# Moving an attention sub-norm's denominators, sums and power from VectorE to GpSimd, and leaving rows unscaled until one last multiply

## The chip, the core and the metric

The kernel runs on one core of a Trainium2 chip. The metric is the device time of one launch in microseconds (us), as the median of several runs. The engines are TensorE (PE in the profile; PEld its weight loads), VectorE (DVE), ScalarE (ACT), GpSimd (POOL), and SyncE (SP), which issues nearly all DMAs. Each engine works through its own list of instructions in order; semaphores tie the lists together.

## The reference, cut to what matters

A two-layer hybrid encoder over 1024 tokens and 16 meta tokens, model width 1024. In each layer half of the width goes through a Fourier mixer, the other half through four heads of differential attention; both are gated and projected back to the residual. What the change touches is the norm of each attention row `o` (128 wide), its gain and its gate:

```python
p = jax.nn.softmax(s, axis=-1)
a = p[:, :, 0] - lam_f * p[:, :, 1]
o = jnp.einsum('bhqk,bkhd->bqhd', a, vf)
...
o = rms_norm(o, subln_gain[li]) * (1.0 - lambda_init)   # o * rsqrt(mean(o*o) + 1e-6) * gain
a_out = o.reshape(b, l, V_WIDTH)
...
y = jnp.concatenate([f_out, a_out], axis=-1)
y = y * jax.nn.silu(gate)
```

## The kernel before

**Stages.** Each layer runs a Fourier stage (`fourier`), then per head a projection from the normed rows (`head_projection`, matmuls on line 545), then attention (`attention`), with other work put between the attention's steps by `fill`: the next head's projection, the projection back of the Fourier half (`out_fourier`) and, towards the end of a layer, that of the attention half (`phase_out`); the latter two share `out_tile` (matmuls L283, addition on DVE L290). Every fp32 operand is split into a high and a low part, and a product takes three matmuls.

**Attention.** A group is two query tiles of 128 rows (and, for the last group of a head in layer 0, the 16 meta rows) of one head; there are 16 groups in each layer. Per tile and for each of the two maps: six scores matmuls into a three-bank PSUM tile "S" (L633, L635); DVE evicts it with its running minimum (L640); ACT takes the exponential with the row's sum (L643). Then DVE takes a reciprocal of the second sum (L647), a factor (L649) and combines both maps into unscaled rows (L651). PE transposes these rows in eight steps and a remainder (L661, L669) into the "M" banks; ACT makes the high part (L666), DVE the low part (L667); the remainder goes through L672 and L673. After a group's last tile PE multiplies with the values (L681, L682) and ACT copies the result (`osb`, L684).

**Finish.** `finish` is called one group later, between later scores. It loads the stored gate (SP, `gt`, L692), transposes the group's output back to rows (PE L695, ACT L697), then works on a set: two tiles (32 sets), or the 16 meta rows alone (4 sets), 36 sets with 68 tile-rows in all. `ls` holds the row sums of the first map. On DVE r1 = 1/ls (L699); on ACT the sum of squares of the rows scaled by r1 (L703, one a tile); on DVE so/128 + eps (L705); on POOL the power of -0.5 (L707); on DVE times r1 (L708); on DVE, one a tile, gate times row times factor (L710); SP stores it (`yad`, L712). `phase_out` loads it back (`ya`, L780), PE transposes it into a "G" bank (L785), and ACT and DVE make high and low parts with the gain column `sgc` (`yh` L789, `yl` L790), which L283 multiplies with the last weights.

**Weights.** `Weights.split` (L172) turns fp32 weights into high (ACT, `wh`, L180) and low parts (DVE, `wl`, L181). They arrive through two staging buffers (`wst`, loads L165), so the third load of a set must wait for both halves of the first to be split.

**Order.** The instructions of each engine aren't in the order of the source. A scheduler with its own model of costs arranges them across all engines before the kernel is built, so an edit in one place can change the order everywhere behind it. PSUM gives three "M" banks, two "G" banks and one "S" tile.

Of the kernel before, what the change touches and what calls it, by code (L numbers as in the profile page):

```python
# [10 lines left out]
F32 = mybir.dt.float32  # L11
F32R = mybir.dt.float32r
AF = mybir.ActivationFunctionType
ALU = mybir.AluOpType
# [4 lines left out]
P = 128  # L19
# [11 lines left out]
EPS = 1e-6  # L31
# [17 lines left out]
def trunk(ctx: ExitStack, tc, x, meta, ngain, w_in, w_f, qg, kg, lq1, lk1, lq2, lk2, subg, w_out,  # L49
          ident_d, chan_d, rope_d, dft_d, dftt_d, out, dbg=None):  # L50
    nc = tc.nc
    pe, act, dve, pool, sp = nc.tensor, nc.scalar, nc.vector, nc.gpsimd, nc.sync
# [4 lines left out]
    sm = ctx.enter_context(tc.tile_pool(name="sm", bufs=3))  # L57
# [7 lines left out]
    def nm(s):  # L65
        uid[0] += 1
        return f"{s}_{uid[0]}"
# [4 lines left out]
    def bank():  # L72
        return psM.tile([P, 512], F32, tag="M", name=nm("M"))
# [22 lines left out]
    def tile_rows(t):  # L96
        return NMETA if t == NT else P
# [13 lines left out]
    sgc = cst.tile([P, DEPTH], F32, name="sgc")  # L111
# [3 lines left out]
    def lam_init(li):  # L115
        return 0.8 - 0.6 * math.exp(-0.3 * li)

    def small_constants(ini):
        W = DEPTH * HD
        lv = [ini.tile([P, 256], F32, tag="sq", name=nm("lv"), bufs=3) for _ in range(2)]  # L120
        for i, v in enumerate((lq1, lk1, lq2, lk2)):
            sp.dma_start(lv[i % 2][:, W * (i // 2):W * (i // 2) + W], v.rearrange("d h -> (d h)").partition_broadcast(P))
        pr = lv[0][:, 0:2 * W].rearrange("p (a c) -> p a c", a=2)
        dve.tensor_tensor(pr, pr, lv[1][:, 0:2 * W].rearrange("p (a c) -> p a c", a=2), op=ALU.mult)
        sums = sm.tile([P, 2 * DEPTH], F32, name="sums", bufs=1)
        dve.tensor_reduce(sums, pr.rearrange("p a (d h) -> p (a d) h", d=DEPTH), axis=AX.X, op=ALU.add)
        act.activation(sums, sums, AF.Exp)
        dve.tensor_tensor(lamb, sums[:, DEPTH:], sums[:, 0:DEPTH], op=ALU.subtract)
        for li in range(DEPTH):
            dve.tensor_scalar(lamb[:, li:li + 1], lamb[:, li:li + 1], lam_init(li), None, op0=ALU.subtract)  # L130
        for dst, g in ((kgc, kg), (qgc, qg)):
            pool.memset(dst, 1.0)
            for c in range(2):
                for li in range(DEPTH):
                    sp.dma_start(dst[HD * c + ROT:HD * c + HD, li:li + 1],
                                 g[li, ROT:HD].rearrange("(h o) -> h o", o=1))
        dve.tensor_scalar(qgc, qgc, HD ** -0.5, None, op0=ALU.mult)
        for li in range(DEPTH):
            sp.dma_start(sgc[:, li:li + 1], subg[li].rearrange("(h o) -> h o", o=1))
            dve.tensor_scalar(sgc[:, li:li + 1], sgc[:, li:li + 1], 1.0 - lam_init(li), 0.5,  # L140
                              op0=ALU.mult, op1=ALU.mult)

    def rope_tables(li, rp, rc):
# [156 lines left out]
    def fourier(li, hT, fo, ep, w, nxt):  # L300
# [116 lines left out]
        for gp in range(2):  # L417
# [20 lines left out]
            if gp == 0:  # L438
                channel_maps()
                with tc.issue_after(ins.ins):  # L440
                    rope_tables(li, ep, fo)
                    if li == 0:
                        small_constants(ep)
# [110 lines left out]
    def attention(li, wk, store, fill, marks, ready, progress):  # L554
# [13 lines left out]
        def group_tiles(gi):  # L568
            return [2 * gi, 2 * gi + 1] + ([NT] if gi == 3 and li < DEPTH - 1 else [])
# [117 lines left out]
        def finish(h, gi, osb, ls):  # L687
            sets = [(0, 2, P)] + ([(2, 1, NMETA)] if len(group_tiles(gi)) > 2 else [])
            for i0, n, R in sets:
                t0 = group_tiles(gi)[i0]  # L690
                gt = wk.tile([P, 2, P], F32, tag="gt", name=nm("gt"), bufs=1)
                sp.dma_start(gt[0:R, 0:n], gtd[li][h][t0:t0 + n, 0:R, :].rearrange("t p d -> p t d"))  # L692
                pb = bank()
                for i in range(n):
                    pe.transpose(pb[0:R, P * i:P * i + P], osb[:, P * (i0 + i):P * (i0 + i) + R], ident)  # L695
                ot = osb[:, 0:2 * P].rearrange("p (t d) -> p t d", t=2)
                act.copy(ot[0:R, 0:n], pb[0:R, 0:P * n].rearrange("p (t d) -> p t d", t=n))  # L697
                r1 = sm.tile([P, 2], F32, tag="r1", name=nm("r1"))
                dve.reciprocal(r1[0:R, 0:n], ls[0:R, i0:i0 + n])  # L699
                so = sm.tile([P, 2], F32, tag="so", name=nm("so"), bufs=2)  # L700
                sqo = wk.tile([P, P], F32, tag="sqo", name=nm("sqo"), bufs=1)
                for i in range(n):
                    act.activation(sqo[0:R], ot[0:R, i], AF.Square, scale=r1[0:R, i:i + 1],  # L703
                                   accum_out=so[0:R, i:i + 1])
                dve.tensor_scalar(so[0:R, 0:n], so[0:R, 0:n], 1.0 / P, EPS, op0=ALU.mult, op1=ALU.add)  # L705
                rs = sm.tile([P, 2], F32, tag="rso", name=nm("rso"), bufs=2)
                pool.tensor_tensor(rs[0:R, 0:n], so[0:R, 0:n], nhalf[0:R, 0:n], op=ALU.pow)  # L707
                dve.tensor_tensor(rs[0:R, 0:n], rs[0:R, 0:n], r1[0:R, 0:n], op=ALU.mult)  # L708
                for i in range(n):
                    dve.scalar_tensor_tensor(gt[0:R, i], ot[0:R, i], rs[0:R, i:i + 1], gt[0:R, i],  # L710
                                             op0=ALU.mult, op1=ALU.mult)
                    sp.dma_start(yad[li][t0 + i][0:R, P * h:P * h + P], gt[0:R, i])  # L712
                    if h == NH - 1:
                        ready.add(t0 + i)
# [6 lines left out]
        def flush_finish():  # L721
            if fin[0] is not None:
                finish(*fin[0])
                fin[0] = None
# [19 lines left out]
        for n, item in enumerate(items):  # L744
            h, gi, i, t = item
# [107 lines left out]
    with tc.tile_pool(name="in0", bufs=2, side="right", reuse_waits="tile") as wk:  # L853
        for t in list(range(MT)) + [NT] + list(range(MT, NT)):
            R = tile_rows(t)
# [145 lines left out]
```

## Time and profile before

| | us |
|---|---|
| median of 3 runs | 1213.92 |
| lowest and highest run | 1213.86, 1215.79 |
| the profiled execution, its own time | 1215.41 |
| its span (first to last instruction) | 1213.6 |
| granted PE clock, mean over the span | 0.994 of full speed |
| PE busy | 1163.2 |
| DVE busy | 833.5 |
| ACT busy | 675.9 |
| POOL busy | 148.5 |

The span is what the views below divide. 1.8 us of the profiled execution's time lie around its span. The table of busy times says which engine has the least room; the waits say whom that engine waited for; the timeline tells, at one place, which instruction stood in front of which.

### The profile page before, as it was taken

The numbers are of one execution on the slowest core, as the hardware profiler recorded it, in microseconds if no ns is written. First come the engines' busy times: TensorE is split into PE (matmuls) and PEld (weight loads), VectorE is DVE, ScalarE is ACT, GpSimd is POOL, SyncE is SP. The second block draws the span as 40 slices with busy tenths as digits, with TensorE's granted clock in tenths as the row PEclk, the third lists the DMA queues.
The fourth block names the chain that finished last, engine by engine and source line by source line (L and its number), as shares of the span: only waits on it lengthen the run. The fifth ranks groups of instructions, "written<-read, shape, count | busy, mean of one in ns | idle before, by whom it ended". The sixth has DMA issues, their size and how long they took to land.

```text
span 1213.6 us, 18701 instructions
## 1 busy us (share of the span) xinstructions
PE 1163.2 (96%) x6676; PEld 1001.6 (83%) x6676; DVE 833.5 (69%) x1803; ACT 675.9 (56%) x1644; POOL 148.5 (12%) x157
## 2 busy tenths in 40 slices
PE   6999999999999999999999999999999999999998
PEld 5999986877787787788879999877888888878786
DVE  6352546788788789888683525367787887987863
ACT  5332325677767667666453223356676776866740
POOL 1101023010211201100011000140111112101000
PEclk9999999999999998999999999999999999999899
DMA  7420303012012014744335202030120210473253
GB/s 236 134 70 18 91 28 101 7 31 77 14 47 61 14 32 148 221 150 131 134 127 167 70 19 90 29 100 8 43 58 23 57 49 20 143 220 128 101 159 117
DMA packets 103613, 105.46 MB, mean 87 GB/s; under 512 B 11233, under 2 KB 87585, under 8 KB 103265
## 3 DMA queue, kind: packets, MB, share of 16 engines
q1 hardware_dynamic: 103104, 99.59, 26.4%
q0 software_dynamic: 416, 4.70, 1.1%
q8 instruction: 52, 0.85, 0.3%
q14 instruction: 41, 0.33, 0.1%
HBM read 74.62 MB, written 29.62 MB: 86 GB/s over the span
## 4 chain that ended last, share of the span: by engine, by line
PE 80%; DVE 8%; ACT 6%; DMA 3%; issue 2%; POOL 1%; SPq 1%; ACTq 0%; DVEq 0%; POOLq 0%
PE G L545 23%; PE G L283 13%; PE G L349 8%; PE S L349 7%; PE M L681 7%; PE S L633 4%; PE S L635 4%; PE M L661 3%; PE S L545 3%; DVE p L640 2%; PE M L390 2%; ACT p L643 2%; DVE p L651 1%; DMA wst<-in_w_in_dram 1%; PE M L401 1%
## 5 line engine op out<-in xcount | busy, mean ns | idle before, releaser
L545 PE MATMUL G<-wh,hT 128*128 128x512 f32 x896 | 307.5, 400 | 2.8 <-ACT va L484 1.0
L545 PEld LDWEIGHTS G<-wh,hT 128*128 128x128 f32 x896 | 167.4, 188 | 42.9 <-ACT wh L180 1.9
L643 ACT ACTIVATE p<-p,mx 128x1040 f32<-128x1040 f32 x136 | 158.6, 1166 | 69.6 <-DVE p L640 68.4
L640 DVE TENSOR_SCALAR_CACHE_REDUCE p<-S 128x1040 f32<-128x1040 f32 x136 | 167.9, 1234 | 40.7 <-PE S L635 33.4
L545 PE MATMUL G<-wl,hT 128*128 128x512 f32 x448 | 176.4, 395 | 0.6 <-DVE wl L181 0.6
L283 PE MATMUL G<-wh,yh 128*128 128x512 f32 (+2 forms) x276 | 107.4, 402 | 6.5 <-ACT yh L789 4.0
L181 DVE TENSOR_TENSOR wl<-wst,wh 128x512 fp32r<-128x512 f32 x128 | 85.7, 701 | 29.5 <-ACT wh L180 29.2
L283 PE MATMUL G<-wl,yh 128*128 128x512 f32 (+2 forms) x276 | 105.8, 392 | 0.0
L180 ACT CAST wh<-wst 128x512 fp32r<-128x512 f32 x128 | 74.7, 620 | 52.5 <-DMA wst<-in_w_in_dram 23.5
L545 PEld LDWEIGHTS G<-wl,hT 128*128 128x128 f32 x448 | 84.3, 188 | 16.3 <-DVE wl L181 1.2
L349 PE MATMUL G<-hT,wh 128*128 128x384 f32 (+3 forms) x384 | 96.4, 331 | 0.0
L283 PE MATMUL G<-wh,yl 128*128 128x512 f32 (+1 forms) x260 | 93.0, 398 | 0.0
L499 POOL TENSOR_TENSOR rsq<-ss,nhalf 128x12 f32<-128x12 f32 x24 | 54.9, 2287 | 307.0 <-DVE ss L497 261.8
L349 PE MATMUL S<-hT,wh 128*128 128x256 f32 (+3 forms) x384 | 91.0, 321 | 1.4 <-DVE sg L437 1.3
L667 DVE TENSOR_TENSOR atl<-M,ath 128x512 fp32r<-128x512 f32 x136 | 86.2, 655 | 5.5 <-ACT ath L666 4.6
L651 DVE SCALAR_TENSOR_TENSOR p<-p,cc,p 128x1040 f32<-128x1040 f32 (+1 forms) x68 | 88.2, 1297 | 1.3
L635 PE MATMUL S<-k,ql 128*128 128x264 f32 (+3 forms) x408 | 88.1, 323 | 0.0
L666 ACT CAST ath<-M 128x512 fp32r<-128x512 f32 x136 | 72.7, 565 | 15.3 <-PE M L661 14.5
L661 PE MATMUL M<-ident,p 128*128 128x128 f32 x544 | 73.8, 271 | 0.1
L681 PE MATMUL M<-ath,vh 128*128 128x256 f32 (+1 forms) x256 | 73.4, 287 | 0.2 <-DVE atl L667 0.2
L681 PE MATMUL M<-ath,vl 128*128 128x256 f32 (+1 forms) x256 | 73.0, 285 | 0.0
L681 PE MATMUL M<-atl,vh 128*128 128x256 f32 (+1 forms) x256 | 72.8, 284 | 0.0
(193 smaller groups left out, 2408.1 us busy)
## 6 DMA issues: line engine op xcount, KB each, us to landing
wst<-in_w_in_dram SPq DMA_DIRECT2D x64, 192.0 KB, 2.8
xt<-in_x_dram SPq DMA_DIRECT2D x16, 512.0 KB, 3.9
wst<-in_w_in_dram SPq DMA_DIRECT2D x32, 256.0 KB, 4.5
wst<-in_w_out_dram SPq DMA_DIRECT2D x16, 512.0 KB, 4.3
xmid<-xt SPq DMA_DIRECT2D x16, 512.0 KB, 2.8
xt<-xmid SPq DMA_DIRECT2D x16, 512.0 KB, 4.6
tab<-in_dft_dram POOLq DMA_DIRECT2D x2, 2096.0 KB, 10.9
yfd<-sg SPq DMA_DIRECT2D x8, 520.0 KB, 2.7
```

What stands on the lines that cost most here:

```text
L180: act.copy(h, self.staged[q][:, j, :])
L181: dve.tensor_tensor(l, self.staged[q][:, j, :], f(h), op=ALU.subtract)
L283: pe.matmul(pb[0:m, 0:e - c], lhsT=a[:, k, 0:m], rhs=b[2 * k + n][:, c:e], start=k == 0 and i == 0, stop=k == 3 and i == n_pass - 1)
L349: pe.matmul(o, lhsT=w[k][:, c:c + P], rhs=hT[:, k, s, a:b], start=k == 0 and i == 0, stop=k == KT - 1 and i == 2)
L545: pe.matmul(pss[t][0:part.shape[-1], a:b], lhsT=part, rhs=w[k][:, a:b], start=k == 0 and i == 0, stop=k == KT - 1 and i == len(pairs) - 1)
L635: ins = pe.matmul(ps[0:R, C0 + a:C0 + b], lhsT=ql[:, qo:qo + R], rhs=kk[:, a:b], start=False, stop=True)
L640: dve.tensor_scalar(pc[0:R], ps[0:R, C0:C0 + L], -1.0, None, op0=ALU.mult, op1=ALU.min, accum_out=mx[0:R])
L643: act.activation(pc[0:R], pc[0:R], AF.Exp, bias=mx[0:R], scale=-1.0, accum_out=lc)
L651: dve.scalar_tensor_tensor(pp[0][0:R], pp[1][0:R], cc[0:R], pp[0][0:R], op0=ALU.mult, op1=ALU.add)
L661: pe.transpose(pb[:, R * j:R * j + R], pa[0:R, P * kt:P * kt + P], ident[0:R, 0:R])
L667: dve.tensor_tensor(atl[:, 4 * c:4 * c + 4, qo:qo + R], src, f(hi), op=ALU.subtract)
L681: pe.matmul(po[:, 0:w], lhsT=v[:, kt, :], rhs=a[:, kt, 0:w], start=kt == 0 and i == 0, stop=False)
```

## The change

Before, the rows were scaled by 1/ls for the sum of squares, and the factor of the norm was multiplied by 1/ls again. Now they stay unscaled: with q the sum of squares of the unscaled row, rsqrt(q/(128 ls²) + eps)/ls equals sqrt(128) · rsqrt(q + 128 · eps · ls²). POOL makes `el` = 128 · eps · ls² in two instructions (L700, L701), adds it to the sum of squares (L706) and raises it to -0.5 (L708); sqrt(128) goes into the constant `sgc` that L789 and L790 apply later. The Square on ACT (now L705) needs no scale. Three DVE instructions a set are gone (L699, L705, L708 of before), three POOL instructions a set are new: 108 of each. The DVE multiplication with the gate (L710) keeps its line.

```diff
-            dve.tensor_scalar(sgc[:, li:li + 1], sgc[:, li:li + 1], 1.0 - lam_init(li), 0.5,
+            dve.tensor_scalar(sgc[:, li:li + 1], sgc[:, li:li + 1], 1.0 - lam_init(li), 0.5 * math.sqrt(P),
...
-                r1 = sm.tile([P, 2], F32, tag="r1", name=nm("r1"))
-                dve.reciprocal(r1[0:R, 0:n], ls[0:R, i0:i0 + n])
+
+                el = sm.tile([P, 2], F32, tag="r1", name=nm("el"))[0:R, 0:n]
+                pool.tensor_tensor(el, ls[0:R, i0:i0 + n], ls[0:R, i0:i0 + n], op=ALU.mult)
+                pool.tensor_scalar(el, el, EPS * P, None, op0=ALU.mult)
                 so = sm.tile([P, 2], F32, tag="so", name=nm("so"), bufs=2)
                 sqo = wk.tile([P, P], F32, tag="sqo", name=nm("sqo"), bufs=1)
                 for i in range(n):
-                    act.activation(sqo[0:R], ot[0:R, i], AF.Square, scale=r1[0:R, i:i + 1],
-                                   accum_out=so[0:R, i:i + 1])
-                dve.tensor_scalar(so[0:R, 0:n], so[0:R, 0:n], 1.0 / P, EPS, op0=ALU.mult, op1=ALU.add)
+                    act.activation(sqo[0:R], ot[0:R, i], AF.Square, accum_out=so[0:R, i:i + 1])
+                pool.tensor_tensor(so[0:R, 0:n], so[0:R, 0:n], el, op=ALU.add)
                 rs = sm.tile([P, 2], F32, tag="rso", name=nm("rso"), bufs=2)
                 pool.tensor_tensor(rs[0:R, 0:n], so[0:R, 0:n], nhalf[0:R, 0:n], op=ALU.pow)
-                dve.tensor_tensor(rs[0:R, 0:n], rs[0:R, 0:n], r1[0:R, 0:n], op=ALU.mult)
```

The change also moves instructions that it doesn't touch, since the scheduler orders all of them anew. The engines' lists are the same up to layer 0's attention; PE keeps all of its instructions, in another order from there on. Three places follow.

On DVE, at the first finish of layer 0 (`att` and `gs` belong to the attention and to the next head's projection, `p_2511` is an eviction of scores):

```order
 L673 TENSOR_TENSOR att<-M_2448,att 16x128
-L705 TENSOR_SCALAR so_2400<-so_2400 128x2
 L480 SCALAR_TENSOR_TENSOR gs_2698<-gs_2698,G_2568 128x128
-L708 TENSOR_TENSOR rso_2405<-rso_2405,r_342_2398 128x2
+L710 SCALAR_TENSOR_TENSOR gt_2392<-osb_2369,rso_2406,gt_2392 128x128 x2
 L640 TENSOR_SCALAR p_2511,mx_2510<-S_2503 128x1040
-L710 SCALAR_TENSOR_TENSOR gt_2392<-osb_2369,rso_2405,gt_2392 128x128 x2
```

The multiplication with the gate moved ahead of the next eviction of scores.

On ACT, late in layer 1, where the last set of weights is split (`wst_12524` and `wst_12534` are the third and the fourth staging load of that set; `yh_12688` is the first tile of `phase_out`):

```order
 L180 CAST wh_12526<-wst_12524 128x512
 L180 CAST wh_12530<-wst_12524 128x512
+L789 ACTIVATE yh_12688<-G_12683,sgc 128x512
+L684 COPY osb_12364<-M_12338 128x256
 L180 CAST wh_12536<-wst_12534 128x512
 L180 CAST wh_12540<-wst_12534 128x512
-L789 ACTIVATE yh_12688<-G_12683,sgc 128x512
-L684 COPY osb_12364<-M_12338 128x256
+L697 COPY osb_12364<-M_12390 128x256
 L643 ACTIVATE p_12416,l_2289_12369<-p_12416,mx_12415 128x1040
-L697 COPY osb_12364<-M_12390 128x256
```

`yh_12688` and the copy of `osb` moved ahead of the two casts of the fourth load.

On DVE at the same place (`wl_12521` is the second half of the second load, whose buffer the fourth load needs):

```order
+L651 SCALAR_TENSOR_TENSOR p_12252<-p_12270,cc_12294,p_12252 128x1040
 L181 TENSOR_TENSOR wl_12521<-wst_11919,wh_12520 128x512
 L290 TENSOR_TENSOR xt_12544<-xt_12544,G_12555 128x512
 L673 TENSOR_TENSOR att<-M_12322,att 16x128
 L290 TENSOR_TENSOR xt_12544<-xt_12544,G_12556 128x512
-L651 SCALAR_TENSOR_TENSOR p_12252<-p_12270,cc_12294,p_12252 128x1040
-L699 RECIPROCAL r_2358_12652<-ls_12242 128x2
 L181 TENSOR_TENSOR wl_12527<-wst_12524,wh_12526 128x512
```

The combination of two maps moved ahead of `wl_12521`, and so ahead of what frees the fourth load's buffer.

## Rows read from the trace of the kernel before

**Rows 1.** The page, busy time, share of the span, instructions of each engine.

```profile
PE 1163.2 (96%) x6676; PEld 1001.6 (83%) x6676; DVE 833.5 (69%) x1803; ACT 675.9 (56%) x1644; POOL 148.5 (12%) x157
```

**Rows 2.** The page, the chain that ended last, share of the span by engine.

```profile
PE 80%; DVE 8%; ACT 6%; DMA 3%; issue 2%; POOL 1%; SPq 1%; ACTq 0%; DVEq 0%; POOLq 0%
```

**Rows 3.** Waits of PE: its line, whom it waited for; us, times, longest.

```profile
PE M L669 <- DVE atl L667: 13.2, 10, 1.8
...
PE S L633 <- DVE p L640: 5.2, 6, 1.4
PE G L283 <- ACT yh L789: 4.0, 2, 2.7
...
PE M L226 <- DVE hT L231: 1.5, 1, 1.5
```

**Rows 4.** Lines of DVE: count | busy us, mean ns | idle before, releasers.

```profile
L640 DVE TENSOR_SCALAR_CACHE_REDUCE p<-S 128x1040 f32<-128x1040 f32 x136 | 167.9, 1234 | 40.7 <-PE S L635 33.4 <-PE M L669 6.3
...
L667 DVE TENSOR_TENSOR atl<-M,ath 128x512 fp32r<-128x512 f32 x136 | 86.2, 655 | 5.5 <-ACT ath L666 4.6
...
L705 DVE TENSOR_SCALAR so<-so 128x2 f32<-128x2 f32 (+1 forms) x36 | 5.7, 159 | 4.1 <-ACT sqo L703 3.8
L699 DVE RECIPROCAL r<-ls 128x2 f32<-128x2 f32 (+1 forms) x36 | 5.7, 158 | 6.8 <-ACT p L643 6.5
...
L708 DVE TENSOR_TENSOR rso<-rso,r 128x2 f32<-128x2 f32 (+1 forms) x36 | 5.5, 154 | 4.3 <-POOL rso L707 4.0
```

**Rows 5.** Lines of POOL, columns as in the group before.

```profile
L707 POOL TENSOR_TENSOR rso<-so,nhalf 128x2 f32<-128x2 f32 (+1 forms) x36 | 26.7, 743 | 332.6 <-DVE so L705 311.0 <-DVE ss L497 21.6
...
L448 POOL TENSOR_TENSOR sg<-sg,yt 128x16 f32<-128x16 f32 x8 | 1.8, 222 | 174.6 <-DVE yt L414 168.1 <-issue 6.5
...
L491 POOL MEMSET ss<- 128x4 f32 x8 | 0.8, 102 | 0.4
```

**Rows 6.** Timeline at 321: start, us, instruction, idle before and its releaser.

```profile
321.10 0.16 DVE L647 RECIPROCAL r<-l 128x1 f32<-128x1 f32 x1 [1.38 <-ACT p L643]
```

**Rows 7.** Timeline at a finish in layer 0.

```profile
250.48 0.16 DVE L708 TENSOR_TENSOR rso<-rso,r 128x2 f32<-128x2 f32 x1 [0.96 <-POOL rso L707]
```

**Rows 8.** Timeline 1137 to 1148, late in layer 1, at the last weights.

```profile
1137.36 1.30 DVE L651 SCALAR_TENSOR_TENSOR p<-p,cc,p 128x1040 f32<-128x1040 f32 x1
...
1138.69 0.60 PE L785 MATMUL G<-ident,ya 128*128 128x128 f32 x4
...
1140.38 1.14 ACT L180 CAST wh<-wst 128x512 fp32r<-128x512 f32 x2 [2.53 <-DMA wst<-in_w_out_dram]
...
1141.42 0.68 ACT L789 ACTIVATE yh<-G,sgc 128x512 fp32r<-128x512 f32 x1
...
1142.15 0.80 PE L283 MATMUL G<-wh,yh 128*128 128x512 f32 x1 [2.75 <-ACT yh L789]
...
1142.25 1.17 ACT L643 ACTIVATE p<-p,mx 128x1040 f32<-128x1040 f32 x1
...
1143.59 1.91 PE L661 MATMUL M<-ident,p 128*128 128x128 f32 x8
```

**Rows 9.** The chain that ended last, two steps of it: start, us, step.

```profile
1135.72 4.58 DMA wst<-in_w_out_dram
...
1151.61 0.87 PE M L661 x8
```

**Rows 10.** Windows: bounds, length, busy of PE, PEld, DVE, ACT, POOL; PEclk, DMA.

```profile
1142.00:1145.00 3.00, 2.85 (x11) 2.55 (x12) 1.36 (x4) 2.20 (x6) 0.00 (x0) 0.50 0.00 0
1145.00:1148.00 3.00, 3.00 (x12) 2.62 (x11) 1.20 (x2) 1.75 (x6) 0.00 (x0) 0.50 0.00 0
1148.00:1150.00 2.00, 2.00 (x9) 1.55 (x9) 2.00 (x4) 1.73 (x5) 0.00 (x0) 0.93 0.00 0
```

**Rows 11.** Timeline at 253.5: a power on POOL beside a DVE instruction.

```profile
253.48 2.27 POOL L499 TENSOR_TENSOR rsq<-ss,nhalf 128x12 f32<-128x12 f32 x1 [3.04 <-DVE ss L497]
253.62 1.30 DVE L651 SCALAR_TENSOR_TENSOR p<-p,cc,p 128x1040 f32<-128x1040 f32 x1
```

## The prediction, written before the changed kernel ran

> **What bounds the kernel now.** I read the busy times first: PE works 1163.2 of 1213.6 us, DVE 69%, ACT 56%, POOL 12% [rows 1]. The chain that ended last agrees: 80% of it is PE, 8% DVE, 6% ACT, 1% POOL [rows 2]. So only the roughly 50 us in which PE does nothing (1213.6 - 1163.2), and stretches with a lowered clock, can be won, and the start and the end of the program hold a good part of those 50. The change takes no work from PE. The next view is therefore whom PE waits for [rows 3]: the low parts of the transposed rows (L667) 13.2 us in 10 places, the eviction of scores (L640) 5.2 in 6, the high part `yh` (L789) 4.0 in 2, of which one place has 2.7, and 1.5 at the end of layer 0. DVE's work appears in 13.2 + 5.2 = 18.4 us of waits. That is all that a lighter DVE could give, and the reader should hold it against the 16.9 us of DVE work that the change removes: the two are not the same us.
>
> **Part 1, VectorE's three instructions a set.** They go away: 5.7 + 5.7 + 5.5 = 16.9 us busy, 36 times each, mean 154 to 159 ns [rows 4]. DVE also idled in front of them, 6.8 + 4.1 + 4.3 = 15.2 us, but that idle time was a wait for ACT or POOL, and what stood behind would often have waited for the same engine. What is the 16.9 worth? At a typical stall of PE, DVE itself had idled 1.38 us for ACT's exponential just before, [rows 6], so DVE being earlier there changes nothing: ACT ends last. At a finish like that of [rows 7] DVE stood 0.96 us for POOL with work behind it, and there a shorter DVE list does help. Of 36 sets two a layer, at a guess, stand directly ahead of one of PE's 16 waits for DVE; each saves 0.16 x 2 or so, 1.0 us or a little more in all. I take **1.0 us**, near the row of 321; the bounds are 0 (ACT ends last everywhere) and 4 (a quarter of the 16.9, since PE waits for DVE in 18.4 of some 830 busy us, concentrated in this stage).
>
> **Part 2, GpSimd's three new instructions a set.** No row shows an add or a multiplication of 128x2 there. The nearest are a fill of 102 ns below and a multiplication of 128x16 of 222 ns above [rows 5]; I take 0.2, near the upper since it also reads two operands. 108 x 0.2 = 22 us on an engine busy 148.5 of 1213.6 [rows 1], hidden. `el` needs only `ls`, known long before, so its two instructions are off the chain of the finish, except where a power of the projection follows: at most 0.45 us late, two or three times. That chain from the squares' end to L710 was 0.16 (L705) + 0.74 (power) + 0.15 (L708) plus hand-overs, about 1.2 us; it becomes 0.2 + 0.74 plus hand-overs, about 1.1. So it is not longer. But it now waits with L710 in DVE's list instead of L708: in the order of the first finish, L710 stands ahead of the eviction of scores. Behind a waiting L710 stand L640 and, through it, ACT's exponential and PE's transposes. In [rows 7] L708 already stood 0.96 there, so I charge **0** here and price the other case as a rival.
>
> The Trainium skill, GPSIMD Engine Reference, section 4.1 Engine selection, speaks against this move: element-wise additions and multiplications belong on VectorE, since GpSimd takes about twice as long with two operands. The trace has no pair of like shapes to test it. By that rule 108 additions take an estimated 2 x 0.16 = 0.31 each, 34 us in place of 22, and the sum below would still be the same as long as POOL is hidden.
>
> **Part 3, the order late in layer 1.** This is the largest term. In [rows 8] ACT stood 2.53 us, to 1140.38, for the last staging load, then cast it (1.14) and only then made `yh` at 1141.42; PE waited 2.75 us for it. After that idling the granted clock was 0.50 from 1142 to 1148, the 1.2 GHz level, and 0.93 in the next window [rows 10]; eight transposes took 1.91 us there against 0.87 later in the chain [rows 8, 9]. The place costs 2.75 + about half of 6 us = 5.7. After the change `yh` stands ahead of the two casts. It then needs only the four transposes that end at 1138.69 + 0.60 = 1139.29, so it is ready at 1139.98 instead of 1142.1, and PE goes on after 0.7 us.
>
> What is late next is the last load: the combination (1.30) [rows 8] has moved ahead of the half that frees its buffer, while 0.3 of removed instructions lies in front, so it starts 1.0 later, at 1136.7, and lands 4.58 later [rows 9], at 1141.3. Its casts end at 1142.45. ACT then copies `osb` (some 0.35) and makes the exponential with its sum (1.17 and some 0.19), to 1144.2. On DVE follow the reciprocal 0.16, an eviction 1.24, the factor 0.2, two low parts 2 x 0.66, the remainder 0.28 and the combination 1.30, in all 4.5 [rows 4, 8]: 1148.7. The transposes of those rows stood at 1151.61 before [rows 9], so the place gives 1151.61 - 1148.65 = **3.0 us**. PE still waits about 2 us in it, in another spot. Bounds: 0, if that later wait again lowers the clock as much, and 5.7, if both wait and low clock go.
>
> **Part 4, the end of layer 0.** The last finish is on the path there: PE waits 1.5 us for the normed rows [rows 3]. L710 of the last group now stands ahead of other work of DVE, and two hand-overs are gone. I take **0.6**, between 0 and the 1.5 of the row, since the loads around it stay.
>
> **Sum.** 1.0 + 0 + 3.0 + 0.6 = 4.6 us. The profiled execution took 1215.41, its span 1213.6; so 1210.8 for a profiled execution after. The median of the runs was 1213.92, 1.5 below it; the forecast against it is 1213.92 - 4.6 = **1209.3 us**. With the lower bounds it is 1213.9, with the upper 1213.92 - (4 + 5.7 + 1.5) = 1202.7.
>
> **Rivals.**
> *Nothing to be had.* The wait at the last weights only changes place, the clock falls behind it as before, and ACT ends last elsewhere. For it: 1.38 us of DVE's idle time ahead of a stall [rows 6]; the later load. Against: `yh` no longer stands behind the casts at all. All terms at their lower bounds: 1212 to 1214.5, I name 1213.5.
>
> *More relief.* The new order loosens PE's waits for DVE in general. 4 us in part 1 and 5 in part 3 give about 1204. For it: all of 18.4 us [rows 3] hang on DVE; against: those are ten-odd places, and most of the sets stand at none of them.
>
> *Slower: L710 stands in DVE's list and holds the eviction.* If in each of the 36 sets nothing covers POOL's addition and power, DVE stands 0.2 + 0.74 = 0.94 us with L640 queued behind it: 34 us, against 16.9 removed and 4.3 of old waits for POOL [rows 4]; 13 us net. PE would see about half of it, as DVE is late in half of its waits: +6.5, and with part 3 lost as well some 1219. It decides from 21.2 / 36 = 0.59 us of standing a set: above that DVE loses. For it: L708's 0.96 wait with [rows 7]. Against: mean idle there was 4.3 / 36 = 0.12 only [rows 4]; the scheduler has usually put work in between.
>
> *A shared port.* In the only overlap that I show, a power of 2.27 on POOL ran from 253.48, and a DVE instruction with two operands, begun 0.14 later, took its ordinary 1.30 [rows 11]. If DVE were held by each of POOL's 108 new instructions in proportion to its own busy share of 69%, DVE would lose 108 x 0.2 x 0.69 = 15 us, all that it won, and with PE seeing a third of it the time were 1213.9 + 5 - 3.6 = 1215.3, a loss. The Trainium skill, SBUF — State Buffer, section Who interferes with whom, has such a rule: a VectorE instruction with two inputs in SBUF and a GpSimd instruction that reads SBUF exclude each other for the whole instruction. By it that DVE row would have ended after 255.75, and the trace shows it ended at 254.92; so it gets a small chance.
>
> **How the numbers follow.** Forecast (1206 to 1211.4) 0.50; nothing to be had 0.22; more relief 0.11; slower by standing 0.14; port 0.03. A measurement here can tell 0.2%, about 2.4 us, from no change; faster then means below 1211.5, slower above 1216.3. The forecast and more relief are faster, 0.61; nothing to be had and most of the port's 1215.3 are the same, 0.24; the rest slower, 0.15. For 8 in 10 the range must reach from the bound of more relief, 1202.7, over nothing to be had to the lower part of the slower case: I take 1203 to 1216. What lies outside is most of the standing case and the tail of relief, 0.17.
>
> **What would show it.** In the profile after: DVE's busy time near 817, POOL's near 170, with 0.1 to 0.25 us for each new instruction. At the last weights PE's wait for `yh` below 1 us, the granted clock near 1.0 behind it, and the transposes some 3 us earlier, relative to the first load's cast; another wait of about 2 us for DVE or ACT shortly after. PE's waits for L667 and L640 a little below 18.4. At the end of layer 0 a wait of about 1. The standing rival would show as idle time of DVE in front of L710 above 21 us with POOL as releaser; the port rival as longer means of L651 and L667-like instructions on DVE. Wrong would be the forecast if PE's idle time is within 1 us of before, or if a new stall above 2 us appears in layer 0, where the order of PE changes from its attention on and I found no term either way.

## The result and the profile after

The changed kernel runs at 1224.04 us, median of 4 runs (1222.88 to 1225.17), against 1214.13 before: a ratio of 1.0082 with an interval of 1.0067 to 1.0098. It was forecast at 1209.3, faster, within 1203 to 1216. It is slower by some 10 us and outside the range.

The first look is again at the busy times and the chain (page of the changed kernel, answering to [rows 1, 2]):

```profile
PE 1164.1 (95%) x6676; PEld 1001.3 (82%) x6676; DVE 824.6 (67%) x1695; ACT 670.2 (55%) x1644; POOL 178.4 (15%) x265
...
PE 73%; DVE 10%; DMA 6%; ACT 5%; issue 3%; SPq 1%; POOL 1%; DVEq 0%; ACTq 0%; POOLq 0%
```

PE does the same 1164 us of work. Its idle time (span less busy) went from 1213.6 - 1163.2 = 50.4 to 1223.0 - 1164.1 = 58.9: that 8.5 us, with 0.9 of busy time, is the whole difference of the spans. DVE and ACT have less to do, by 8.9 and 5.7 us, POOL 29.9 more. So three engines that do not bound the kernel changed as intended, or nearly, and the one that does waits longer. For whom (waits of PE in the changed kernel; line, whom it waited for, us, times, longest; compare [rows 3]):

```profile
PE M L669 <- DVE atl L667: 15.7, 10, 2.8
...
PE S L633 <- DVE p L640: 8.2, 9, 1.9
...
PE G L545 <- ACT va L484: 2.2, 1, 2.2
...
PE G L283 <- ACT yh L789: 1.0, 2, 0.7
...
PE M L226 <- DVE hT L231: 0.5, 1, 0.5
```

Two waits that the forecast meant to shrink did: for `yh` from 4.0 to 1.0, at the end of layer 0 from 1.5 to 0.5. But the waits for DVE's low parts and evictions, 18.4 before, are 23.9, although DVE has less work. To find where, I set the kernels side by side by the ends of DVE's combinations (L651), of which there are 68 in both. But for two that come earlier in the changed kernel, the two kernels are within 0.3 us of each other up to the twelfth, at 335; they are 5.0 us apart at 419, 10.5 at 507, 10.5 to 12.8 between there and 1044, 13.5 at 1124, and 9.4 at the end. The first two stretches, before and after, each ending at the same combination (windows: bounds, length, busy time of PE, PEld, DVE, ACT, POOL, granted clock, DMA share and GB/s):

```profile
335.30:418.90 83.60, 79.29 (x464) 65.37 (x462) 66.73 (x151) 59.17 (x148) 12.10 (x10) 1.00 0.15 41
418.90:507.10 88.20, 84.99 (x469) 69.25 (x470) 76.85 (x171) 62.67 (x151) 8.39 (x8) 0.96 0.40 118
```

```profile
335.20:423.90 88.70, 82.44 (x466) 67.95 (x464) 66.53 (x142) 58.93 (x150) 15.47 (x23) 0.96 0.14 39
423.90:517.60 93.70, 85.39 (x469) 69.46 (x470) 76.38 (x156) 62.75 (x151) 13.86 (x23) 0.96 0.36 108
```

The reader sees the same matmuls, but for two in the first stretch, in 5.1 and 5.5 us more. The loss sits in layer 0, at the ends of the first and the second head, a place on which the forecast has no term. In the first stretch the granted clock fell as well (0.96 against 1.00, two stretches of 3.4 us at 0.50, the 1.2 GHz level). Over the whole span the clock is the same: 0.994 on average in both.

One stall of the second stretch, line by line (timeline of the changed kernel; start, us, instruction, idle before it and its releaser):

```profile
451.43 1.09 PE L661 MATMUL M<-ident,p 128*128 128x128 f32 x8
...
452.54 1.16 ACT L643 ACTIVATE p<-p,mx 128x1040 f32<-128x1040 f32 x1
...
453.70 1.05 ACT L666 CAST ath<-M 128x512 fp32r<-128x512 f32 x2
453.83 0.16 DVE L647 RECIPROCAL r<-l 128x1 f32<-128x1 f32 x1 [0.79 <-ACT p L643]
...
454.28 1.30 DVE L651 SCALAR_TENSOR_TENSOR p<-p,cc,p 128x1040 f32<-128x1040 f32 x1
...
455.50 1.28 DVE L667 TENSOR_TENSOR atl<-M,ath 128x512 fp32r<-128x512 f32 x2
456.24 0.28 PE L669 MATMUL M<-ident,p 128*16 128x128 f32 x1 [2.77 <-DVE atl L667]
```

and the same instructions in the kernel before:

```profile
446.39 1.04 PE L661 MATMUL M<-ident,p 128*128 128x128 f32 x8
...
447.58 1.08 ACT L666 CAST ath<-M 128x512 fp32r<-128x512 f32 x2
448.30 0.69 DVE L667 TENSOR_TENSOR atl<-M,ath 128x512 fp32r<-128x512 f32 x1
...
448.50 0.27 PE L669 MATMUL M<-ident,p 128*16 128x128 f32 x1
448.68 1.17 ACT L643 ACTIVATE p<-p,mx 128x1040 f32<-128x1040 f32 x1
```

None of these instructions belongs to the change, and none takes more than 0.05 us longer. They stand in another order: the exponential (L643) is now ahead of the casts of the transposed rows (L666), and the combination (L651) ahead of the low parts (L667) that PE waits for. PE waits 2.77 us where it did not wait.

### The profile page after: what moved, and what is told of

Same layout as the page of the kernel before. It is cut to its first block, busy times and chain, and to the rows that moved or that the text cites. A ratio compares the mean times of both kernels' runs of the same rounds, so it can differ in the third digit from the quotient of the medians.

```text
span 1223.0 us, 18719 instructions
## 1 busy us (share of the span) xinstructions
PE 1164.1 (95%) x6676; PEld 1001.3 (82%) x6676; DVE 824.6 (67%) x1695; ACT 670.2 (55%) x1644; POOL 178.4 (15%) x265
## 4 chain that ended last, share of the span: by engine, by line
PE 73%; DVE 10%; DMA 6%; ACT 5%; issue 3%; SPq 1%; POOL 1%; DVEq 0%; ACTq 0%; POOLq 0%
PE G L545 22%; PE G L283 12%; PE G L349 7%; PE M L681 7%; PE S L349 6%; PE S L633 4%; PE S L635 4%; PE S L545 3%; PE M L661 3%; DVE p L640 2%; DMA wst<-in_w_in_dram 2%; PE M L390 2%; ACT p L643 2%; DVE p L651 1%; DVE atl L667 1%
## 5 line engine op out<-in xcount | busy, mean ns | idle before, releaser
L643 ACT ACTIVATE p<-p,mx 128x1040 f32<-128x1040 f32 x136 | 158.5, 1166 | 75.5 <-DVE p L640 73.1
L640 DVE TENSOR_SCALAR_CACHE_REDUCE p<-S 128x1040 f32<-128x1040 f32 x136 | 167.9, 1235 | 40.9 <-PE S L635 36.5
L651 DVE SCALAR_TENSOR_TENSOR p<-p,cc,p 128x1040 f32<-128x1040 f32 (+1 forms) x68 | 88.3, 1298 | 1.7
L667 DVE TENSOR_TENSOR atl<-M,ath 128x512 fp32r<-128x512 f32 x136 | 86.0, 655 | 3.7 <-ACT ath L666 2.8
L666 ACT CAST ath<-M 128x512 fp32r<-128x512 f32 x136 | 72.9, 563 | 13.3 <-PE M L661 12.3
```

What stands on the lines that cost most here:

```text
L640: dve.tensor_scalar(pc[0:R], ps[0:R, C0:C0 + L], -1.0, None, op0=ALU.mult, op1=ALU.min, accum_out=mx[0:R])
L643: act.activation(pc[0:R], pc[0:R], AF.Exp, bias=mx[0:R], scale=-1.0, accum_out=lc)
L651: dve.scalar_tensor_tensor(pp[0][0:R], pp[1][0:R], cc[0:R], pp[0][0:R], op0=ALU.mult, op1=ALU.add)
L667: dve.tensor_tensor(atl[:, 4 * c:4 * c + 4, qo:qo + R], src, f(hi), op=ALU.subtract)
```

## The experiments

**Work and order, apart.** Theory O says that the new order is the loss; theory W, that it is the instructions: L710 now stands in DVE's list waiting for GpSimd, and GpSimd and DVE get in each other's way. A small addition to a kernel pins every engine's list to a table of instruction numbers:

```diff
+    named = {i.name: i for i in nc.cur_bb.bb.instructions}
+    for order in table.values():
+        own = [named[f"I-{n}"] for n in order]
+        for a, b in zip(own, own[1:]):
+            tc.add_manual_dep(b, a.name, info, reason="pin")
...
         trunk(tc, *args)
+        _pin(nc, tc)
```

The instructions that only one of the kernels has are not in the table and go where the scheduler puts them. First the changed kernel's instructions in the old order:

> The changed kernel's instructions, but every engine issues those that both kernels have in the order of the kernel before; the GpSimd instructions that are new go where their data allow. Theory O (the order): what the change lost, 9.9 us, came with the scheduler's new order in layer 0, and the instructions themselves save a little, since DVE's busy time fell by 8.9 us and ACT's by 5.7; so this runs at 1210 to 1214 us. Theory W (the work): the multiplication with the gate now stands in DVE's list waiting for GpSimd (idle time in front of it rose from 0.4 to 7.5 us), and GpSimd's instructions collide with DVE's; then the loss stays, 1220 us or more.

Measured: 1213.75 us, ratio to the kernel before 1.0001 (0.9991 to 1.0011). The loss is gone. Then the other way round:

> The kernel before, with its own instructions on DVE and GpSimd, but every engine issues those that both kernels have in the order of the changed kernel. Theory O: the loss comes along without the change's instructions, 1222 to 1226 us. Theory W: close to the kernel before, 1212 to 1217 us.

Measured: 1234.71, ratio 1.0172 (1.0151 to 1.0193). With the medians of the first comparison and of this one:

| | old order | new order |
|---|---|---|
| old instructions | 1214.1 to 1214.5 | 1234.7 |
| new instructions | 1213.75 | 1224.0 |

Theory O holds, and more strongly than it said: the order costs 10 us with the new instructions and 20 with the old. The new instructions alone are worth nothing measurable in the old order and 10 us in the new one. So what the removed DVE instructions are worth depends on the order they stand in. At one place the traces show how. Behind the same gate product and split of weights, PE waits 2.16 us with the new instructions and 3.10 with the old, because the old ones have DVE stand for GpSimd's power in front of both; here the old ones in the new order (timeline):

```profile
373.19 0.16 DVE L708 TENSOR_TENSOR rso<-rso,r 128x2 f32<-128x2 f32 x1 [0.59 <-POOL rso L707]
...
375.13 0.28 DVE L480 SCALAR_TENSOR_TENSOR gs<-gs,G 128x128 f32<-128x128 f32 x1
...
375.44 0.37 ACT L481 COPY qk<-G 128x256 f32<-128x256 f32 x1 [0.99 <-DVE gs L480]
...
376.83 0.50 PE L545 MATMUL G<-wh,hT 128*128 128x512 f32 x1 [3.10 <-ACT va L484]
```

Where the rest of the 10.7 us between them lies was not followed up. In the traces the two are as far behind the kernel before at 507 (10.5 and 11.0 us, old ones second), and part only behind it (10.2 and 16.9 at the last combination).

**Which part of the order.** The two orders agree, as sets of instructions behind them, at many places, so they can be joined there. First the second stretch alone:

> The changed kernel's instructions in the order of the kernel before, but in the new order between 419 and 507 us of the trace of the kernel before (layer 0, its second and third heads). Theory O says that this stretch alone loses: 93.7 us against 88.2, so 5 us above the run with the old order throughout, with a wait of PE for DVE's low parts (L667) above 2 us in it. If the loss is spread, or comes of the two orders meeting, under 2 us.

Measured: 1219.54, ratio 1.0044 (1.0029 to 1.0059), 5.8 above the old order throughout (5.2 by the ratios). The stall is there, as long as in the changed kernel (timeline of this run):

```profile
450.96 0.38 PE L669 MATMUL M<-ident,p 128*16 128x128 f32 x1 [2.77 <-DVE atl L667]
```

> The changed kernel's instructions in the order of the kernel before, but in the new order between 335 and 419 us of the trace of the kernel before (layer 0, where the first head ends and the second begins). The run with the new order from 419 to 507 alone lost 5 us, and in the traces 335 to 419 lost as much (88.7 against 83.6). If each stretch loses by itself, 1218 to 1220 us; if that first loss was only the phase of the clock, which fell twice there in the changed kernel and not in the kernel before, 1213 to 1215.

Measured: 1216.57, ratio 1.0022 (1.0008 to 1.0036): 2.8 above the old order, between the two expectations. The profiled execution took 1213.63 and had no lowered clock before 1210. Between the same two combinations it shows (window of this run):

```profile
336.10:421.40 85.30, 79.03 (x464) 65.51 (x462) 65.80 (x141) 58.53 (x149) 15.46 (x23) 1.00 0.15 40
```

So in this execution, with the clock up, the new order loses 1.7 us here against the 83.60 before, and not 5.1. In the changed kernel the two stretches of 3.4 us at 0.50 cost, by an estimate, up to half of their length each, 3.4 us; that is the rest. The waits are the same (1.99 and 2.15 us here, 2.03 and 2.16 there): they are followed by the lower clock in some executions and not in others. The ten times of this run go roughly with it, from 1213.6 at a mean clock of 1.000 over 1217.6 to 1217.8 at 0.994 to 1219.5 at 0.993.

> The changed kernel in its own new order, but in the order of the kernel before between 335 and 507 us of the trace of the kernel before. If these two stretches hold the loss, 1224 - 2 x 5 = 1213 to 1215 us, or less with the gain at the last weights (3.4 us as measured). If the new order loses everywhere a little, above 1218.

Measured: 1213.59, ratio 1.0002 (0.9991 to 1.0013), that is 10.4 below the changed kernel. The two stretches, 14% of the program, hold the loss. The rest of the new order is not free either: against 1211.06 of a run below, which is old up to 1124 and new from there, it costs 2.5 (3.6 by the ratios).

**Single places in line.** Two of the stalls in these stretches can be mended by hand without touching the rest of the new order. At the one shown above:

```diff
 ACT  L619 qa
-ACT  L643 p
 ACT  L666 ath x2
+ACT  L643 p
...
 DVE  L620 ql
-DVE  L647 r, L649 cc, L651 p
 DVE  L667 atl x2
+DVE  L647 r, L649 cc, L651 p
```

and likewise at 354, where L666 stood behind L618 and L619, and L667 behind L651, L492 and L620.

> The changed kernel in its own new order, but for two local moves in layer 0, at the stalls of 2.03 and 2.77 us in which PE waited for the low parts of transposed rows (L667). At both, ACT's two casts of the high parts (L666) go ahead of two copies of queries, or of an exponential, and DVE's two low parts (L667) go ahead of a combination (L651). If these few places in line are what PE waited for, most of 2.03 + 2.77 us comes back: 1219 to 1222 us. If the wait only moves on to the next thing that is late, 1223 to 1225.

Measured: 1217.46, ratio 1.0026 (1.0011 to 1.0041): 6.6 us of the 10 came back, more than the stalls' 4.8. The waits are (timeline of this run):

```profile
352.97 0.28 PE L669 MATMUL M<-ident,p 128*16 128x128 f32 x1 [0.79 <-DVE atl L667]
...
449.26 0.28 PE L669 MATMUL M<-ident,p 128*16 128x128 f32 x1 [0.43 <-DVE atl L667]
```

2.03 and 2.77 became 0.79 and 0.43, which is 3.6 us; the rest goes with other waits (PE's idle time fell by 5.6, from 58.9 to 53.3) and with the clock: the changed kernel's lowered stretches at 355.7 and 376.2 are missing in this execution, and its mean is 0.997 against 0.994.

**GpSimd and L710.** Theory W's two mechanisms, tried by themselves. In the old order, with the square made twice and half of it added twice:

```diff
-                pool.tensor_tensor(el, ls[0:R, i0:i0 + n], ls[0:R, i0:i0 + n], op=ALU.mult)
-                pool.tensor_scalar(el, el, EPS * P, None, op0=ALU.mult)
+                for _ in range(2): pool.tensor_tensor(el, ls[0:R, i0:i0 + n], ls[0:R, i0:i0 + n], op=ALU.mult)
+                pool.tensor_scalar(el, el, EPS * P / 2, None, op0=ALU.mult)
...
-                pool.tensor_tensor(so[0:R, 0:n], so[0:R, 0:n], el, op=ALU.add)
+                for _ in range(2): pool.tensor_tensor(so[0:R, 0:n], so[0:R, 0:n], el, op=ALU.add)
```

> The changed kernel's instructions in the order of the kernel before, with two more instructions on GpSimd a set: the square of the row sum is made twice, and half of it is added twice, so the chain from the squares to the factor is one addition longer (0.28 to 0.31 us as measured), 36 times. If GpSimd and its chain are hidden, as in the run with the old order, 1213 to 1215 us. If the multiplication with the gate standing in DVE's list costs PE time, 36 x 0.3 = 11 us on DVE, and 3 us or more on the time: 1217 or above.

Measured: 1213.96, ratio 1.0005 (0.9994 to 1.0016). POOL is busy 202.0 us instead of 183.9, and neither that nor the longer chain shows in the time: the idle time in front of L710 rose by 0.7 us in all, to 4.6. This was tried in the old order only. Then L710's place in line, in the changed kernel with the two moves:

```diff
-DVE  L710 gt x2
 DVE  L181 wl x2
 DVE  L480 gs
 DVE  L640 p
+DVE  L710 gt x2
```

> The changed kernel in its new order with the two local moves of the run before (1217.5 us), and at two more places (372 and 472 us of its trace) DVE's pair of multiplications with the gate (L710) goes behind two splits of weights, a gate product and an eviction of scores. If L710 standing early in DVE's list holds the eviction that PE waits 1.95 us for, 0.6 us come back at each place, 1216 to 1217; if it is not L710, nothing does, 1217 to 1219.

Measured: 1217.91, ratio 1.0032 (1.002 to 1.0045), 0.4 above the run without this move: nothing came back in the time. L710 did hold the eviction, as supposed: PE's wait for it at the second place fell from 1.95 to 1.43 us. But the next wait, for L667, grew from 0.75 to 1.29, so L710's early place isn't what sets the time there. With the splits of weights behind L480 and L640 as well:

> As the run with the two local moves (1217.5 us), and at the same two further places the gate product (L480) and the eviction of scores (L640) go ahead of L710's pair and of the two splits of weights (L181) together, which takes 1.9 us away from in front of them on DVE. If place in DVE's list is what is left of the loss, the waits of 2.1 and 1.95 us shrink by over 1 us each and the time to 1213.5 to 1216; if ACT ends last there, 1217 to 1219.

Measured: 1216.17, ratio 1.0024 (1.0012 to 1.0036), 1.3 below the run with the two moves by the medians, and by the ratios (1.0024 against 1.0026) not below it: no gain that can be told. The wait for the eviction at 475 is gone, but the next one took its place (timeline of this run):

```profile
471.69 0.38 PE L669 MATMUL M<-ident,p 128*16 128x128 f32 x1 [2.49 <-DVE atl L667]
```

Which order is right for the remaining 2 to 4 us of these stretches stays open; it was not tried further.

**The last weights.** The largest term of the forecast, on its own:

> The changed kernel's instructions in the order of the kernel before up to 1124 us of its trace, and in the new order behind that, where the wait for the last weights stands. Theory O, with the step on the last weights right: from there to the end the changed kernel was 4.1 us quicker than the kernel before (85.0 against 89.1), so 1209 us, some 4 below the run with the old order throughout. If that gain hung on the phase in which the new order of layer 0 left the clock, no difference from the old order throughout.

Measured: 1211.06, ratio 0.9972 (0.9959 to 0.9984). This version beats both kernels. It does what the forecast described (timeline of this run; compare [rows 8]):

```profile
1136.85 1.14 ACT L180 CAST wh<-wst 128x512 fp32r<-128x512 f32 x2 [2.49 <-DMA wst<-in_w_out_dram]
...
1137.89 0.68 ACT L789 ACTIVATE yh<-G,sgc 128x512 fp32r<-128x512 f32 x1
...
1138.63 0.50 PE L283 MATMUL G<-wh,yh 128*128 128x512 f32 x1 [0.68 <-ACT yh L789]
...
1139.41 1.04 PE L661 MATMUL M<-ident,p 128*128 128x128 f32 x8
```

PE waits 0.68 for `yh`, the clock stays up, and eight transposes take 1.04 us where they took 1.91. (The cast at 1136.85 is that of the third load, the one at 1140.38 in [rows 8] that of the fourth; the fourth's stands behind `yh` here, at 1138.86.) The same order with the old instructions:

> The instructions of the kernel before, in its own order up to 1124 us of its trace and in the new order behind that, where the wait for the last weights stands. The changed kernel's instructions in these orders took 1211.1 us. If the order of the casts alone gives the gain, 1209.5 to 1212 us with the old instructions too; if the three instructions fewer on DVE are needed for it, 1213 to 1216.

Measured: 1215.46, ratio 1.0011 (0.9999 to 1.0023). No gain. The profiled execution, of 1216.36, shows the stall again (timeline; the combination L651 is the last one ahead of the place where the two orders are joined):

```profile
1124.49 1.30 DVE L651 SCALAR_TENSOR_TENSOR p<-p,cc,p 128x1040 f32<-128x1040 f32 x1
...
1128.92 0.62 DVE L710 SCALAR_TENSOR_TENSOR gt<-osb,rso,gt 128x128 f32<-128x128 f32 x2
...
1134.86 3.82 SPq L165 DMA_DIRECT2D wst<-in_w_out_dram  x2
...
1141.08 1.14 ACT L180 CAST wh<-wst 128x512 fp32r<-128x512 f32 x2 [3.93 <-DMA wst<-in_w_out_dram]
...
1142.86 0.55 PE L283 MATMUL G<-wh,yh 128*128 128x512 f32 x1 [2.16 <-ACT yh L789]
```

With the new instructions the corresponding rows are:

```profile
1121.74 1.30 DVE L651 SCALAR_TENSOR_TENSOR p<-p,cc,p 128x1040 f32<-128x1040 f32 x1
...
1125.91 0.61 DVE L710 SCALAR_TENSOR_TENSOR gt<-osb,rso,gt 128x128 f32<-128x128 f32 x2
...
1131.83 3.90 SPq L165 DMA_DIRECT2D wst<-in_w_out_dram  x2
```

It looks as if L710 and the load came 3.0 us earlier by the shorter chain of the change. But 2.75 of that is between the two executions already at L651, ahead of the new order. Counted from L651, L710 comes 0.26 and the third load's issue 0.28 us earlier with the new instructions. Its cast begins 5.02 us behind the issue, against 6.22 with the old ones. So of the 1.48 us by which `yh` and PE's wait for it differ, 0.3 can be the change's, and 1.2 is a load that took longer to land; in the other twelve traces this load takes 4.2 to 5.0 us from issue to landing. Why it was late here no run shows.

By the times, this joined order gains with the new instructions and not with the old (ratios 0.9972 and 1.0011); that the shorter chain is the reason is not shown. Nor does the gain need the new instructions in general. Against that speaks the run with the old instructions in the new order throughout (timeline of `old_work_new_order`):

```profile
1156.08 1.14 ACT L180 CAST wh<-wst 128x512 fp32r<-128x512 f32 x2 [0.58 <-DMA wst<-in_w_out_dram]
...
1159.71 0.50 PE L283 MATMUL G<-wh,yh 128*128 128x512 f32 x1 [0.66 <-ACT yh L789]
```

There PE waits 0.66 us for `yh` with the old instructions as well, and from the same combination to the end it takes 86.3 us, against 85.0 in the changed kernel and 89.1 in the kernel before. The order brings most of the gain there. In both joined runs the third load goes out later behind that combination's end than in the whole new order, 8.8 and 9.1 us against 7.3 and 7.6, so joining the orders has a price of its own. The eleven times of the joined run with the old instructions lie between 1210.9 and 1216.7, and the trace is of one near the top.

## Why the prediction was wrong, point by point

**What bounds the kernel.** Right, and it is what shows the loss: PE's work stayed, its waits grew. The sentence that DVE's 16.9 us and PE's 18.4 us of waits "are not the same us" was more right than meant: in the old order the work is worth nothing that can be measured.

**The step that failed** is the sum itself. It adds the terms of four parts and takes every other place where the order changes as 0; the last sentence names layer 0, "where the order of PE changes from its attention on and I found no term either way", and leaves it out. That term, put at nothing without a reason, was some +10: 10.4 by the kernel without the two stretches, 2.8 + 5.8 = 8.6 by the two stretches one by one, with waits of PE for L667 of 2.03 and 2.77 us, and in the first stretch the lower clock behind them in some executions. The prediction's own sign of being wrong, a new stall above 2 us in layer 0, came true. It could have been looked for: in the order of the two kernels, ahead of L667, one sees at 354 and 452 an exponential, a combination or a copy of queries come in front, and [rows 8] price the exponential at 1.17 and the combination at 1.30 us in front of what PE waits for.

**Part 1**, DVE's three instructions. No gain can be measured in the old order (ratio 1.0001); a gain of 1.0 would lie within the interval (0.9991 to 1.0011), so the term is neither borne out nor refuted. Its basis was mis-sized: 108 instructions of 154 to 159 ns are 16.9 us in sum, but DVE's busy time fell by 8.9. Part of each lies over the next instruction (timeline of the kernel before):

```profile
1138.58 0.16 DVE L699 RECIPROCAL r<-ls 128x2 f32<-128x2 f32 x1
1138.65 1.27 DVE L181 TENSOR_TENSOR wl<-wst,wh 128x512 fp32r<-128x512 f32 x2
```

The next began 0.07 us after L699. And ACT gained what the forecast did not count: the Square without a scale (L705, before L703) takes 314 ns instead of 406, 68 times, 6.3 us.

**Part 2**, GpSimd. 0.2 a piece was right for an undisturbed instruction and low for the mean, 0.28 to 0.31; that it is hidden was right, and `pool_more` shows it in the old order. (The title counts the power among what moved; it stood on GpSimd before, too, as L707.)

**Part 3**, the last weights. Right in mechanism, and near in size: 4.1 us in the changed kernel's trace against 3.0; by the run with the new order only there 2.7 (1213.75 - 1211.06), 3.5 by the ratios. The load was said to start 1.0 us later and to land 4.58 later. In the changed kernel the fourth load's issue does come 1.1 later, counted from the end of the last combination ahead (12.36 us against 11.22). But it lands 3.6 us behind its issue, so in the end only 0.1 later, and the wait of about 2 us that the forecast kept for another spot was 0.71 (timeline of the changed kernel):

```profile
1150.35 0.33 SPq L165 DMA_DIRECT2D wst<-in_w_out_dram  x1
...
1153.93 1.14 ACT L180 CAST wh<-wst 128x512 fp32r<-128x512 f32 x2 [0.15 <-DMA wst<-in_w_out_dram]
...
1160.87 1.09 PE L661 MATMUL M<-ident,p 128*128 128x128 f32 x8 [0.71 <-DVE p L651]
```

**Part 4**, the end of layer 0: the wait fell from 1.5 to 0.5, 1.0 against 0.6.

**The rivals.** The slower one had the right sign and the wrong mechanism. L710's row on DVE, before and after (count | busy us, mean ns | idle before, releasers):

```profile
L710 DVE SCALAR_TENSOR_TENSOR gt<-osb,rso,gt 128x128 f32<-128x128 f32 (+1 forms) x68 | 20.9, 344 | 0.4
```

```profile
L710 DVE SCALAR_TENSOR_TENSOR gt<-osb,rso,gt 128x128 f32<-128x128 f32 (+1 forms) x68 | 20.9, 346 | 7.5 <-POOL rso L708 3.1 <-DMA out_dram<-xt 2.0 <-DMA gt<-gtd 1.9
```

Of the 7.5 us of idle time 3.1 are for POOL, against the rival's price of 34 and the 21 from which it decides, and neither lengthening the chain nor moving L710 changed the time. The port rival did not come about; the last section has the rows, and what the forecast's row could not show. What happened, a scheduler's new order for instructions the change doesn't touch, was no rival with a chance, and that made the range too narrow.

## What to carry to other kernels

Where a scheduler orders the program, a small edit is two changes, the instructions and the order, and the second can be several times the first: pin one and measure the other. Compare the order ahead of each instruction that the bounding engine waits for, before summing what the edit saves. And two timelines are compared from the last point at which both did the same, not by their absolute times: a difference of 3.0 us was 2.75 already before the place in question.

## What the runs showed of the hardware

A GpSimd addition that starts while DVE runs an instruction with two operands in SBUF is held until that one ends. The addition L706 takes 0.19 us beside an eviction (at 446.15) and 0.85 beside a combination (timeline of the changed kernel):

```profile
368.74 1.30 DVE L651 SCALAR_TENSOR_TENSOR p<-p,cc,p 128x1040 f32<-128x1040 f32 x1
...
369.25 0.85 POOL L706 TENSOR_TENSOR so<-so,el 128x2 f32<-128x2 f32 x1 [11.19 <-ACT sqo L705]
```

Of 36 in the changed kernel 31 took 180 to 198 ns and 5 took 695 to 937. Six began while L651 ran; the five long ones are among them, and the sixth began 0.14 us before its end.

The other way round, no DVE instruction is seen to be held by the change's new instructions: L651's mean is 1298 ns against 1297 before. But a longer GpSimd instruction that both kernels have, a multiplication of 128x1024, does hold DVE (timeline of the changed kernel):

```profile
160.10 2.44 POOL L447 TENSOR_TENSOR sg<-sg,yt 128x1024 f32<-128x1024 f32 x1
160.20 2.46 DVE L513 TENSOR_TENSOR r<-qk,sgt 128x96 f32<-128x96 f32 x1
...
162.59 0.24 DVE L514 TENSOR_TENSOR r<-qk,sgt 128x96 f32<-128x96 f32 x1
```

L513 began 0.10 us after it and lasted until it ended; L514, of the same shape, took 0.24. The power of [rows 11] did not do this, and it was the only row on which the forecast judged the port rival: it tells of the power, not of additions and multiplications. The Trainium skill, SBUF — State Buffer, section Who interferes with whom, has the rule that a VectorE instruction with two SBUF inputs and a GpSimd instruction that reads SBUF exclude each other, whoever comes first; the traces agree with it for the addition that came second and for the multiplication that came first, and not for the power, beside which L651 took its ordinary 1.30 us.

The Trainium skill's GPSIMD Engine Reference, section 4.1 Engine selection, puts element-wise work with two operands at about twice VectorE's time on GpSimd. At 128x2 the trace shows less: an undisturbed multiplication (L700) took 0.19 us on GpSimd, against the 154 ns mean of L708 on DVE before [rows 4].
